# Order of the small fp32 and fp32r matrix products in a hybrid attention block: outputs grouped by type, transposes taken in pairs

## The chip, the cores and the metric

The kernel runs on one core of one Trainium2 chip. The metric is the device time of one execution in microseconds (us); less is better. The time of the kernel before is the median of three runs. One further execution was taken with the hardware profiler; times "in the trace" count from the start of its span.

Engines are named as the profile does: PE is TensorE's matrix products and PEld its weight loads, DVE is VectorE, ACT ScalarE, POOL GpSimd, SP SyncE, which issues most DMA transfers.

## What is computed

One decoder layer on 272 tokens (16 meta tokens and 256 inputs) of width 2048, in fp32: a normalised input goes through one wide projection; two token mixers work side by side; their outputs are gated, summed and projected; then comes an MLP. The change touches the two mixers only. Cut from the reference:

```python
def gated_linear_attention(q, k, v, g):          # 4 heads, key width 256, value width 512, chunks of 64
    b = jnp.cumsum(gc, axis=3)
    q_dec = qc * jnp.exp(b)
    k_inv = kc * jnp.exp(-b)
    k_end = kc * jnp.exp(b_last - b)
    a = jnp.where(causal, jnp.einsum('bhnck,bhnsk->bhncs', q_dec, k_inv), 0.0)
    o_intra = jnp.einsum('bhncs,bhnsv->bhncv', a, vc)
    ...
def forgetting_attention(q, k, v, f_logit, b_forget):   # 8 heads of width 128
    s = jnp.einsum('bhqd,bhkd->bhqk', qh, kh) * scale + c[q] - c[k]
    p = jax.nn.softmax(jnp.where(mask, s, MASK_VALUE), axis=-1)
    outs.append(jnp.einsum('bhqk,bhkd->bhqd', p, vh))
```

The kernel writes the first as a quadratic attention over all 256 queries with decays folded into keys and queries: a score matrix at0/at1/az times the values.

## The kernel before

**Precision.** Large products are made from split operands: a number is cut into a high part in the type fp32r (a copy on ScalarE) and the rest (a subtraction on VectorE), and three, or for some shapes two, fp32r products are added up in PSUM. Small products are made in plain fp32; each of these shows as two records in the trace (its weights in two halves). A transpose is a product with the identity and shows as one record.

**The stream.** TensorE works through 128-column blocks of the weights. For each, `next_weights` loads two halves (SP), copies the high part `whi` (ScalarE, L120) and subtracts to get `wlo` (VectorE, L121); there are five buffers of halves. `gemm_all` (L148, L150, L152) makes 48 products of 272 columns for all tokens into a PSUM tile `psa`; `gemm2` (L143, L144) makes 16 pairs of 512 and 256 columns into `ps`. Both draw on a pool of three PSUM banks (`pg`); small products draw on one of five (`px`).

**The order.** Work between the large products is registered with `later(n, fn)`: `fn` is written into the program after the n-th following large product (`issued()` counts). From this program a scheduling pass makes the order of each engine's instructions, and an instruction may be placed earlier or later than it was written; the order is fixed when the kernel is built, and each engine takes its instructions in that order.

**A head of the linear attention** (`gla_head`) uses, in order: two key blocks, two query blocks (for head 0 the first key block and the queries come from the start-up stage), four value blocks, and for heads 1 to 3 four gate blocks. Its small work:

- `keys` (L519, L521) reads the key block's PSUM tile and writes the scaled keys `kx` and `kz`; L534, L538 and L540 scale queries and keys further (`qx`, `kx`).
- `scores` (L557, ten fp32 products into `pa`), registered with `later(3)` ahead of the value blocks.
- each value block i is read from PSUM into `vT` (L598, VectorE; the tag `vT` has two buffers, so the third block's write waits until the first block's transposes have read theirs), and `turn(i)` (L586, L587; for the last block also L590) transposes it into the PSUM tiles p0 and p1.
- `outputs` (L612, and L201 to L203 by way of `three`, L620), `sums` and `scale`.

`decays(hd)` (L415 to L446), one for each head, makes the factors `eb_all` and `en_all` that the keys and queries are multiplied with, by a long row of ScalarE and VectorE operations; head 0's runs while head 0's value blocks are on TensorE.

**A head of the softmax attention** (`fox_head`) uses a key, a query and a value block. `turn_v` (L769, L770) transposes the values, `turn_p` (L779 to L781) the probabilities, `out_v` (L201 to L203, L788) multiplies them.

Of the kernel before, what the change touches and what calls it, by code (L numbers as in the profile page):

```python
# [16 lines left out]
P = 128  # L17
# [3 lines left out]
NT = 256  # L21
# [44 lines left out]
def trunk(ctx: ExitStack, tc: tile.TileContext, hT, w_small, w_all, consts, w_alpha2, out):  # L66
    nc = tc.nc
    serial = [0]

    def nm(s):  # L70
        serial[0] += 1
        return f"{s}_{serial[0]}"
# [7 lines left out]
    px = ctx.enter_context(tc.tile_pool(name="px", bufs=5, space=PSUM))  # L80
# [3 lines left out]
    def bank(pool, s):  # L84
        return pool.tile([P, 512], F32, tag="bank", name=nm(s))
# [4 lines left out]
    def later(n, fn):  # L90
        waiting.append([n, fn])
# [33 lines left out]
    def next_weights(keep_hi=None):  # L125
        c = chunk[0]
        chunk[0] += 1
        parts = []
        for i in range(2):
            hi, lo, step = weight_half(c, i, None if keep_hi is None else keep_hi[:, HK * i : HK * (i + 1), :])  # L130
            step(0, HK)
            parts.append((hi, lo))
        return lambda k: (parts[k // HK][0][:, k % HK, :], parts[k // HK][1][:, k % HK, :])
# [29 lines left out]
    def gemm_all(w):  # L163

        ps = bank(pg, "psa")
        for k in range(KT):
            hi, lo = w(k)
            mac3(ps, hi, lo, k, k == 0, k == KT - 1)
        join(ps)
        issued()  # L170
        return ps
# [15 lines left out]
    def split_to(dst_hi, dst_lo, src):  # L187
        nc.scalar.copy(dst_hi, src)
        nc.vector.tensor_tensor(dst_lo, src, dst_hi.bitcast(F32), op=ALU.subtract)

    def split(pool, tag, src, bufs=None):

        kw = {} if bufs is None else {"bufs": bufs}
        hi = pool.tile(list(src.shape), F32R, tag=tag + "h", name=nm(tag + "h"), **kw)
        lo = pool.tile(list(src.shape), F32R, tag=tag + "l", name=nm(tag + "l"), **kw)
        split_to(hi, lo, src)
        return hi, lo

    def three(out, lhs, rhs, first, last):

        nc.tensor.matmul(out, lhs[0], rhs[0], start=first, stop=False)  # L201
        nc.tensor.matmul(out, lhs[0], rhs[1], start=False, stop=False)
        nc.tensor.matmul(out, lhs[1], rhs[0], start=False, stop=last)  # L203
# [279 lines left out]
    def padded(pool, name, cols, dtype=F32):  # L483
        t = pool.tile([P, cols], dtype, name=name)
        nc.gpsimd.memset(t if dtype == F32 else t.bitcast(F32), 0.0)
        return t

    Q1 = 2 * C - NM
    NB = NA - 4 * C
    at0 = padded(lin, "at0", NT)  # L490
    at1 = padded(lin, "at1", NT - Q1)
    vg = padded(lin, "vg", P)
    az = padded(lin, "az", 4 * NB)
    v0 = [lin.tile([P, GLA_DV], F32R, name=n) for n in ("v0h", "v0l")]
# [8 lines left out]
    def gla_head(hd, sg, ready=None):  # L503
# [74 lines left out]
        v1 = att.tile([P, GLA_DV], F32, tag="v1", name=nm("v1"))  # L578
# [3 lines left out]
        def turn(i, vT):  # L582
            if not pv:
                pv.extend(bank(px, s) for s in ("p0", "p1"))
            cols = slice(P * i, P * (i + 1))
            nc.tensor.transpose(pv[0][:, cols], vT[:, 0:P], ident)  # L586
            nc.tensor.transpose(pv[1][:, cols], vT[:, P : 2 * P], ident)  # L587
            if i == 3:
                p2 = bank(px, "p2")[:, 0:P]
                nc.tensor.transpose(p2, vg, ident)  # L590
                split_to(*v0, pv[0])
                nc.scalar.copy(v1, pv[1])
                nc.scalar.copy(vz, p2)

        for i in range(4):
            ps = gemm_all(next_weights())
            vT = tmp.tile([P, NA], F32, tag="vT", name=nm("vT"))
            nc.vector.tensor_tensor(vT, ps[:, 0:NA], rb, op=ALU.mult)  # L598
            nc.gpsimd.tensor_copy(vg[:, NB * i : NB * (i + 1)], vT[:, 4 * C :])
            later(1, lambda i=i, vT=vT: turn(i, vT))  # L600


        oT = att.tile([P, 4, NT], F32, tag="oT", name=nm("oT"))
# [4 lines left out]
        def outputs():  # L608
            a0 = split(att, "a0", at0)
            cz = so[:, 3, 0 : 4 * NB]  # L610
            pz = bank(px, "po")[:, 0 : 4 * NB]
            nc.tensor.matmul(pz, vz, az, start=True, stop=True)  # L612
            nc.scalar.copy(cz, pz)
            for i in range(2):
                po = bank(px, "po")
                for j in range(2):
                    v = slice(P * (2 * i + j), P * (2 * i + j + 1))
                    o = po[:, NT * j : NT * (j + 1)]
                    three(o, [e[:, v] for e in v0], a0, True, False)
                    nc.tensor.matmul(o[:, Q1:], v1[:, v], at1, start=False, stop=True)  # L620
                pj = po.rearrange("p (j t) -> p j t", t=NT)
                zj = pj[:, :, NT - NB :]
                nc.vector.tensor_tensor(zj, zj, cz.rearrange("p (j t) -> p j t", t=NB)[:, 2 * i : 2 * i + 2, :],
                                        op=ALU.add)
                nc.scalar.copy(oT[:, 2 * i : 2 * i + 2, :], pj)
                nc.scalar.activation(so[:, 2 * i : 2 * i + 2, :], pj, AF.Square)
            nc.gpsimd.tensor_tensor(so[:, 0:2, :], so[:, 0:2, :], so[:, 2:4, :], op=ALU.add)
            nc.gpsimd.tensor_tensor(so[:, 0, :], so[:, 0, :], so[:, 1, :], op=ALU.add)
# [4 lines left out]
        def scale():  # L633
            for i in range(4):
# [4 lines left out]
                split_to(og_tile()[:, j, 0, :], og_tile()[:, j, 1, :], oT[:, i, :])  # L639

        later(2, outputs)
        later(3, sums)
        if sg is None:
# [36 lines left out]
    for hd in range(GLA_H):  # L680
        later(1 + 3 * hd, lambda hd=hd: with_table(decays, hd))
    later(3 * GLA_H - 1, lambda: with_table(forget))
    gla_head(0, sg0, (qd0, first_ps[NF - 1]))
    for hd in range(1, GLA_H):
        gla_head(hd, None)
# [27 lines left out]
    def fox_head(hd):  # L713
# [38 lines left out]
        vT = tmp.tile([P, NA], F32, tag="vT", name=nm("vT"))  # L752
# [56 lines left out]
                      for o in range(2))  # L809
            split_to(hi, lo, og4)  # L810

        later(1, turn_v)
        later(2, turn_p)
        later(3, out_v)
        if four == 3:
# [2 lines left out]
    for hd in range(FOX_H):  # L818
        fox_head(hd)
# [97 lines left out]
    for n in range(NL):  # L917
        j, ps = KT - NL + n, bank(pg if n < 3 else px, "ps")
# [149 lines left out]
```

## Time and profile before

| | |
|---|---|
| median of three runs | 1538.71 us (1538.29 to 1539.51) |
| the profiled execution | 1538.62 us |
| its span, first to last instruction | 1536.8 us |
| granted TensorE clock, mean | 0.999 |
| instructions of the four compute engines and weight loads | 25427 |
| first output product (L612) of heads 0 and 3 of the linear attention | 95.0 and 292.4 us into the span |
| first score product (L736) of the softmax heads, last product of their last correction (L805) | 326.8 and 479.1 us |

The page of the profile gives busy time by engine, the chain of work that ended last, and the costliest groups. A matmul's record is longer than the time for which it holds TensorE: it includes the way through the array, and the next one starts before it ends. So costs of small products are read from the distance between starts, and the record's length only where two records are drawn together ("x2").

The stretch that the change touches ends at about 479 us. In it TensorE is busy nearly throughout; the gaps between large products hold the small ones: the outputs of head 3 run from 292.44 to 294.97 us, the transposes of one value block hold a gap of a few tenths of a microsecond.

### The profile page before, as it was taken

The page shows a single profiled execution, that of the slowest core. Times are in us where ns is not written, and L with a number is a line of the kernel's source. Part 1 is how long each engine was busy: PE and PEld are TensorE (multiplying, and loading weights), DVE is VectorE, ACT ScalarE, POOL GpSimd, SP SyncE. Part 2 cuts the span into 40 slices and gives each one's busy share as a digit, 9 for nine tenths or more (in the row PEclk, how much of TensorE's full clock was granted, in tenths as well). Part 3 has the DMA queues.
Part 4 walks back from the last instruction along what each step waited for, and adds up shares of the span by engine and source line. Part 5 has one row for each costly group of instructions (what it writes and reads, how often), then busy time and mean ns, then how long its engine had stood idle before and what let it go on. Part 6 is the DMA issues. An engine that isn't in the chain of part 4 may idle for free.

```text
span 1536.8 us, 25427 instructions
## 1 busy us (share of the span) xinstructions
PE 1525.6 (99%) x9812; PEld 1402.4 (91%) x9812; DVE 1059.5 (69%) x1659; ACT 789.6 (51%) x1271; POOL 127.6 (8%) x213
## 2 busy tenths in 40 slices
PE   9999999999999999999999999999999999999997
PEld 8999999999999999999999899999999999999997
DVE  7898858586666656556777876567765776667765
ACT  6766444555545444444655554445444454444563
POOL 6012000011100000000011000000000000000022
PEclk9999999999999999999999999999999999999999
DMA  9455545465555655666565556666565666656652
GB/s 325 165 165 165 182 161 188 157 210 173 167 166 182 201 195 199 197 198 200 182 212 195 193 195 201 195 200 196 194 202 196 201 196 197 199 195 201 192 192 101
DMA packets 86602, 293.09 MB, mean 191 GB/s; under 512 B 9112, under 2 KB 16800, under 8 KB 86352
## 3 DMA queue, kind: packets, MB, share of 16 engines
q1 hardware_dynamic: 85872, 289.62, 57.6%
q8 instruction: 77, 1.26, 0.3%
q0 software_dynamic: 176, 1.12, 0.2%
q10 hardware_dynamic: 432, 0.72, 0.1%
q14 instruction: 45, 0.37, 0.1%
HBM read 289.32 MB, written 2.11 MB: 190 GB/s over the span
## 4 chain that ended last, share of the span: by engine, by line
PE 97%; DVE 1%; ACT 1%; issue 0%; POOL 0%; DMA 0%; POOLq 0%; ACTq 0%; DVEq 0%
PE ps L143 51%; PE ps L144 26%; PE psa L152 5%; PE psa L148 5%; PE psa L150 4%; PE ps L359 1%; PE ps L361 1%; PE ps L937 1%; PE pa L557 1%; PE ps L921 0%; DVE wlo L121 0%; ACT whi L120 0%; PE po L620 0%; DMA h<-hT_dram 0%; POOL o L985 0%
## 5 line engine op out<-in xcount | busy, mean ns | idle before, releaser
L121 DVE TENSOR_TENSOR wlo<-raw,whi 128x1024 fp32r<-128x1024 f32 x522 | 640.3, 1227 | 400.0 <-ACT whi L120 390.8
L120 ACT CAST whi<-raw 128x1024 fp32r<-128x1024 f32 x522 | 546.9, 1048 | 604.7 <-PE ps L143 534.0
L143 PE MATMUL ps<-x,whi 128*128 128x512 f32 x1952 | 656.4, 382 | 0.8 <-DVE x L874 0.8
L144 PE MATMUL ps<-x,wlo 128*128 128x256 f32 x1952 | 535.3, 274 | 0.0
L143 PEld LDWEIGHTS ps<-x,whi 128*128 128x128 f32 x1952 | 366.4, 188 | 64.2 <-DVE x L874 1.1
L144 PEld LDWEIGHTS ps<-x,wlo 128*128 128x128 f32 x1952 | 366.4, 188 | 0.1
L143 PE MATMUL ps<-a,whi 128*128 128x512 f32 x960 | 320.0, 380 | 0.0
L144 PE MATMUL ps<-a,wlo 128*128 128x256 f32 x960 | 262.4, 274 | 0.0
L143 PEld LDWEIGHTS ps<-a,whi 128*128 128x128 f32 x960 | 179.9, 188 | 30.8
L148 PE MATMUL psa<-x,whi 128*128 128x272 f32 x640 | 182.5, 286 | 0.0
L152 PE MATMUL psa<-x,whi 128*128 128x272 f32 x640 | 180.8, 283 | 0.0
L144 PEld LDWEIGHTS ps<-a,wlo 128*128 128x128 f32 x960 | 180.2, 188 | 0.3
L150 PE MATMUL psa<-x,wlo 128*128 128x272 f32 x624 | 176.3, 283 | 0.0
L148 PEld LDWEIGHTS psa<-x,whi 128*128 128x128 f32 x640 | 120.0, 187 | 0.3
L152 PEld LDWEIGHTS psa<-x,whi 128*128 128x128 f32 x640 | 120.0, 187 | 0.0
L150 PEld LDWEIGHTS psa<-x,wlo 128*128 128x128 f32 x624 | 117.2, 188 | 0.0
L862 POOL TENSOR_TENSOR acc<-acc,hsq 128x256 f32<-128x256 f32 x26 | 28.4, 1092 | 736.4 <-ACT hsq L861 736.4
L143 PE MATMUL ps<-og,whi 128*128 128x512 f32 x256 | 85.8, 380 | 0.0
L143 PE MATMUL ps<-y,whi 128*128 128x512 f32 x256 | 85.3, 380 | 0.0
L144 PE MATMUL ps<-og,wlo 128*128 128x256 f32 x256 | 70.2, 274 | 0.0
L144 PE MATMUL ps<-y,wlo 128*128 128x256 f32 x256 | 70.0, 274 | 0.0
L184 DVE TENSOR_TENSOR evt<-ps,evb 128x256 f32<-128x256 f32 x158 | 65.9, 417 | 0.5 <-ACT evb L181 0.5
(297 smaller groups left out, 1420.9 us busy)
## 6 DMA issues: line engine op xcount, KB each, us to landing
raw<-w_all_dram SPq DMA_DIRECT2D x537, 512.0 KB, 4.3
raw<-w_all_dram SPq DMA_DIRECT2D x8, 384.0 KB, 6.7
h<-hT_dram SPq DMA_DIRECT2D x8, 275.0 KB, 6.8
negc<-fdram POOLq DMA_DIRECT2D x1, 1088.0 KB, 7.9
out_dram<-o SPq DMA_DIRECT2D x2, 512.0 KB, 2.6
raw<-w_all_dram SPq DMA_DIRECT2D x2, 256.0 KB, 3.7
room<-w_small_dram SPq DMA_DIRECT2D x1, 320.0 KB, 7.9
out_dram<-o ACTq DMA_DIRECT2D x1, 320.0 KB, 3.0
```

The costliest lines, as they stand in the source:

```text
L120: nc.scalar.copy(hi[:, k, :], r)
L121: nc.vector.tensor_tensor(lo[:, k, :], r, hi[:, k, :].bitcast(F32), op=ALU.subtract)
L143: nc.tensor.matmul(steps(ps), hi, steps(row(x)), start=first, stop=False)
L144: nc.tensor.matmul(steps(ps[:, 0:NT]), lo, steps(x[:, 0, :]), start=False, stop=last)
L148: nc.tensor.matmul(steps(ps[:, X_LO]), hi, steps(x_lo[:, k]), start=first, stop=False, skip_group_check=True)
L150: nc.tensor.matmul(steps(ps[:, 0:NA]), lo, steps(x_hi[:, k]), start=False, stop=last and hi is None, skip_group_check=True)
L152: nc.tensor.matmul(steps(ps[:, 0:NA]), hi, steps(x_hi[:, k]), start=False, stop=last, skip_group_check=True)
L184: nc.vector.tensor_tensor(t, ps[:, 0:NT], b, op=ALU.add)
L359: nc.tensor.matmul(steps(ps), hi, steps(row(x[:, k])), start=st, stop=False)
L361: nc.tensor.matmul(steps(ps[:, 0:NT]), lo, steps(x[:, k, 0]), start=False, stop=sp)
L557: nc.tensor.matmul(dst, k[:, a], q[:, a, :], start=(a == 0), stop=(a == 1))
L862: nc.gpsimd.tensor_tensor(acc, acc, sq, op=ALU.add)
```

## The change

Three edits, with no change to what is computed:

1. The transposes of value blocks 0 and 2 wait for one more large product, so that blocks 0 and 1, and blocks 2 and 3, are transposed in the same gap.
2. `outputs` makes all twelve fp32r products of a head first, into two PSUM tiles (`pos`), then the fp32 product `pz` and then the four fp32 products with `at1`. Only the first product into a tile's bank carries the start flag. Before, each of the four output quarters had three fp32r products followed by its fp32 product, and `pz` came first.
3. `turn_v` of the softmax heads waits for one more large product and so comes into the gap of `turn_p`.

```diff
-            later(1, lambda i=i, vT=vT: turn(i, vT))
+            later(2 - i % 2, lambda i=i, vT=vT: turn(i, vT))
...
             a0 = split(att, "a0", at0)
             cz = so[:, 3, 0 : 4 * NB]
+            pos = [bank(px, "po") for _ in range(2)]
+            parts = [(slice(P * n, P * (n + 1)), pos[n // 2][:, NT * (n % 2) : NT * (n % 2 + 1)], n % 2) for n in range(4)]
+            for v, o, j in parts:
+                for n, (e, b) in enumerate(((v0[0], a0[0]), (v0[0], a0[1]), (v0[1], a0[0]))):
+                    nc.tensor.matmul(o, e[:, v], b, start=(j == 0 and n == 0), stop=False, skip_group_check=True)
             pz = bank(px, "po")[:, 0 : 4 * NB]
             nc.tensor.matmul(pz, vz, az, start=True, stop=True)
             nc.scalar.copy(cz, pz)
-            for i in range(2):
-                po = bank(px, "po")
-                for j in range(2):
-                    v = slice(P * (2 * i + j), P * (2 * i + j + 1))
-                    o = po[:, NT * j : NT * (j + 1)]
-                    three(o, [e[:, v] for e in v0], a0, True, False)
-                    nc.tensor.matmul(o[:, Q1:], v1[:, v], at1, start=False, stop=True)
+            for v, o, j in parts:
+                nc.tensor.matmul(o[:, Q1:], v1[:, v], at1, start=False, stop=True, skip_group_check=True)
+            for i, po in enumerate(pos):
                 pj = po.rearrange("p (j t) -> p j t", t=NT)
...
-        later(1, turn_v)
+        later(2, turn_v)
         later(2, turn_p)
```

The scheduling pass makes new orders from this. Three places follow. Names carry their buffer's number; lines behind the output products are one higher in the changed kernel.

TensorE in head 0, before, at the end of the fourth value block (`psa_136_1036`). `psa_150_1110` is the first key block of head 1:

```order
L152 MATMUL psa_136_1036<-x_81,whi_134_1031 128x4x17x4
L586 MATMUL p0_112_902<-cons_82,vT_129_1021 128x128
L587 MATMUL p1_113_903<-cons_82,vT_129_1021 128x128
L148 MATMUL psa_150_1110<-x_81,whi_145_1099 128x4x17x4
L150 MATMUL psa_150_1110<-x_81,wlo_146_1100 128x4x17x4
```

Thirty products into that key block later, still before, the scores stand:

```order
L152 MATMUL psa_150_1110<-x_81,whi_148_1105 128x4x17x4
L557 MATMUL pa_128_1001<-qx_79_663,kx_77_661 64x48
L148 MATMUL psa_150_1110<-x_81,whi_148_1105 128x4x17x4
L150 MATMUL psa_150_1110<-x_81,wlo_149_1106 128x4x17x4
L557 MATMUL pa_128_1001<-qx_79_663,kx_77_661 64x48
L557 MATMUL pa_128_1001<-qx_79_663,kx_77_661 64x64 x2
```

The same place now; in brackets the engine whose semaphore the instruction waits for. `vT_103_835` and `vT_112_902` are value blocks 0 and 1, `psa_150_1108` is the key block of head 1:

```order
L152 MATMUL psa_136_1036<-x_81,whi_134_1031 128x4x17x4
L557 MATMUL pa_126_997<-qx_79_663,kx_77_661 64x48 [waits DVE_49]
L586 MATMUL p0_127_1015<-cons_82,vT_103_835 128x128 [waits DMAHW1_49]
L587 MATMUL p1_128_1016<-cons_82,vT_103_835 128x128
L586 MATMUL p0_127_1015<-cons_82,vT_112_902 128x128
L587 MATMUL p1_128_1016<-cons_82,vT_112_902 128x128
L557 MATMUL pa_126_997<-qx_79_663,kx_77_661 64x48 [waits DVE_49]
L557 MATMUL pa_126_997<-qx_79_663,kx_77_661 64x64 x2
L557 MATMUL pa_126_997<-qx_79_663,kz_78_662 64x16 [waits Pool_49]
L557 MATMUL pa_126_997<-qx_79_663,kz_78_662 64x16 [waits DVE_49]
L148 MATMUL psa_150_1108<-x_81,whi_145_1097 128x4x17x4 [waits Activation_49]
```

The first score product has moved from inside the key block to directly behind the fourth value block, ahead of the transposes of the first two value blocks; the key block's 48 products all come behind the ten small score products.

VectorE in head 0, before, in the queue ahead of the `kx` that these scores read (`half_92_745`, `room_83`, `ends_538` belong to `decays`, `vT_129_1021` is value block 2):

```order
L440 TENSOR_TENSOR room_83<-room_83,half_92_745 128x2x256
L598 TENSOR_TENSOR vT_129_1021<-psa_121_921,rb_534 128x272
L436 TENSOR_TENSOR ends_538<-ends_538 128x2
L121 TENSOR_TENSOR wlo_155_1174<-raw_153_1172,whi_154_1173 128x1024
L424 TENSOR_SCALAR room_83<-pz_123_973,cons_82 128x272
```

and now:

```order
L440 TENSOR_TENSOR room_83<-room_83,half_92_745 128x2x256
L436 TENSOR_TENSOR ends_538<-ends_538 128x2
L121 TENSOR_TENSOR wlo_155_1174<-raw_153_1172,whi_154_1173 128x1024
L424 TENSOR_SCALAR room_83<-pz_121_969,cons_82 128x272
L424 TENSOR_SCALAR room_83<-pz_122_970,cons_82 128x272
```

The read of value block 2 has left this place; it now stands behind both L519 and L540, and waits for TensorE. The other operations up to `kx` are the same, with one weight split and one small addition (L176) in another place among them.

TensorE at the outputs of head 1, before (`po_1885` here is the tile of `pz`):

```order
L612 MATMUL po_1885<-az,vz_1443 128x64
L201 MATMUL po_1888<-a0h_1881,v0h 128x256
L202 MATMUL po_1888<-a0l_1882,v0h 128x256
L201 MATMUL po_1900<-a0h_1881,v0h 128x256
L203 MATMUL po_1888<-a0h_1881,v0l 128x256
L620 MATMUL po_1888<-at_545,v_193_1442 128x144
L201 MATMUL po_1888<-a0h_1881,v0h 128x256
L202 MATMUL po_1888<-a0l_1882,v0h 128x256
L203 MATMUL po_1888<-a0h_1881,v0l 128x256
L620 MATMUL po_1888<-at_545,v_193_1442 128x144
```

and now, the end of the same row:

```order
L615 MATMUL po_1886<-a0h_1881,v0h 128x256
L615 MATMUL po_1886<-a0l_1882,v0h 128x256
L615 MATMUL po_1886<-a0h_1881,v0l 128x256
L617 MATMUL po_1899<-az,vz_1443 128x64
L620 MATMUL po_1885<-at_545,v_193_1442 128x144 x2
L620 MATMUL po_1886<-at_545,v_193_1442 128x144 x2
L143 MATMUL ps_1933<-x,whi_1922 128x4x32x4
```

The five fp32 products of the head (L617, four times L620) stand together behind the twelve fp32r ones.

## The prediction

> **What bounds the kernel now.** I read the page first: busy times, then the chain of work that ended last.
>
> ```profile
> PE 1525.6 (99%) x9812; PEld 1402.4 (91%) x9812; DVE 1059.5 (69%) x1659; ACT 789.6 (51%) x1271; POOL 127.6 (8%) x213
> PE 97%; DVE 1%; ACT 1%; issue 0%; POOL 0%; DMA 0%; POOLq 0%; ACTq 0%; DVEq 0%
> ```
>
> TensorE is the bound: whatever is added to its row, work or idle time, is added to the span, and nothing later can take it back. So the next view is the one of waits, for TensorE alone.
>
> ```profile
> PE warm L323 <- DVE ones L208: 1.3, 1, 1.3
> PE ps L143 <- DVE x L874: 0.8, 1, 0.8
> PE pn L961 <- ACT sq L942: 0.7, 1, 0.7
> PE ps L359 <- ACT whi L292: 0.4, 1, 0.4
> PE pa L557 <- DVE kx L519: 0.3, 1, 0.3
> ```
>
> Of these five waits one lies where the change works: the first score product of head 0 (L557) waits for VectorE's scaled keys kx (L519). The window view of the stretch ahead of it shows why (the columns are length, then busy time of TensorE, weight load, VectorE, ScalarE, GpSimd, then granted clock):
>
> ```profile
> 67.60:83.80 16.20, 15.86 (x128) 15.42 (x127) 15.92 (x33) 12.24 (x23) 3.66 (x4) 1.00 0.50 164
> ```
>
> VectorE is busy 15.92 of 16.20 us. It is an average of 69% over the kernel, but here it has a queue with no room, and what stands in that queue ahead of kx sets when kx exists. TensorE is full as well only because the order gives it other products until then.
>
> **The change at that place.** TensorE now, in order of time (timeline):
>
> ```profile
> 73.29 0.33 PE L586 MATMUL p<-cons,vT 128*128 128x128 f32 x1
> ...
> 79.33 0.29 PE L152 MATMUL psa<-x,whi 128*128 128x272 f32 x1
> 79.45 0.27 PE L586 MATMUL p<-cons,vT 128*128 128x128 f32 x1
> 79.56 0.27 PE L587 MATMUL p<-cons,vT 128*128 128x128 f32 x1
> 79.59 0.37 PE L148 MATMUL psa<-x,whi 128*128 128x272 f32 x1
> 79.80 0.29 PE L150 MATMUL psa<-x,wlo 128*128 128x272 f32 x1
> ...
> 83.23 0.29 PE L152 MATMUL psa<-x,whi 128*128 128x272 f32 x1
> 83.82 0.31 PE L557 MATMUL pa<-qx,kx 128*64 128x48 f32 x2 [0.30 <-DVE kx L519]
> 84.06 0.39 PE L148 MATMUL psa<-x,whi 128*128 128x272 f32 x1
> 84.29 0.28 PE L150 MATMUL psa<-x,wlo 128*128 128x272 f32 x1
> 84.50 0.56 PE L557 MATMUL pa<-qx,kx 128*64 128x48 f32 x6
> ```
>
> The fourth value block of head 0 ends at 79.45. Then come two transposes and 30 products of the next head's first key block, 79.59 to 83.35, and only then the scores. In the changed order (shown above) the first score product stands directly behind the fourth value block, ahead of all 48 products of that key block. TensorE takes its matmuls in order, so those products can no longer cover the time until kx. VectorE:
>
> ```profile
> 72.80 0.43 DVE L598 TENSOR_TENSOR vT<-psa,rb 128x272 f32<-128x272 f32 x1
> ...
> 77.22 0.43 DVE L598 TENSOR_TENSOR vT<-psa,rb 128x272 f32<-128x272 f32 x1
> 77.57 0.15 DVE L436 TENSOR_TENSOR ends<-ends 128x2 f32<-128x2 f32 x1
> ...
> 83.35 0.42 DVE L519 TENSOR_TENSOR kx<-ps,en_all 128x256 f32<-128x256 f32 x1
> ```
>
> *When TensorE gets there.* A pair of transposes with its change of type costs 79.80 − 79.45 − 0.12 (the L148's own, from 79.33 to 79.45 for the same shape) = 0.23 us. Three pairs stood ahead of 79.45, the third just behind it; the first, at the end of the second block, goes, but its 0.23 turns into waiting: the fourth block's first product needs the buffer that the L598 of 72.80 + 0.43 = 73.23 empties, the same event for which the L586 of 73.29 waits now. The second pair's 0.23 is gained. So the fourth block ends at 79.45 − 0.23 = 79.22.
>
> *When kx is there.* The same queue stands ahead of kx, less the L598 of 77.22, which now waits for transposes: 77.57 − 77.22 = 0.35 us. kx is written by 83.35 + 0.42 − 0.35 = 83.42, and L557 starts 0.05 later, as now (83.77, 83.82): 83.47.
>
> *The stall* is 83.47 − 79.22 = 4.25 us. Now it is 83.82 − (83.23 + 0.12) = 0.47. With the first pair's 0.23 turned into waiting: 4.25 − 0.47 + 0.23 = **+4.0 us**. Behind it TensorE has its usual work. ScalarE and VectorE come out further ahead of it, which helps nothing. If VectorE's reordered small operations cost or save 0.1, so does the stall; from 3.8 to 4.2.
>
> **What it saves.** Scores: two records alone now take 84.29 − 0.12 − 83.82 = 0.35; the ten that follow take 85.41 − 0.12 − 84.50 = 0.79, 0.08 each:
>
> ```profile
> 85.19 0.39 PE L152 MATMUL psa<-x,whi 128*128 128x272 f32 x1
> 85.41 0.28 PE L148 MATMUL psa<-x,whi 128*128 128x272 f32 x1
> ```
>
> In the new order they follow each other among other fp32 products: 0.35 − 0.16, **−0.2** (0 to −0.3).
>
> Outputs, four heads:
>
> ```profile
> 292.44 0.33 PE L612 MATMUL po<-az,vz 128*128 128x64 f32 x2
> ...
> 292.77 0.29 PE L202 MATMUL po<-a0l,v0h 128*128 128x256 f32 x1
> 292.89 0.28 PE L201 MATMUL po<-a0h,v0h 128*128 128x256 f32 x1
> ...
> 293.73 0.41 PE L620 MATMUL po<-at,v 128*128 128x144 f32 x2
> ...
> 294.10 0.28 PE L203 MATMUL po<-a0h,v0l 128*128 128x256 f32 x1
> ```
> ```profile
> L620 PE MATMUL po<-at,v 128*128 128x144 f32 x32 | 6.5, 286 | 0.0
> ```
>
> An fp32 product with the fp32r one behind it takes 294.10 − 293.73 = 0.37; less the fp32r product's 0.12 (292.77 to 292.89) that is 0.25. Its two records of 286 ns lie 0.41 − 0.29 = 0.12 apart, so without a change of type it would take 0.24 to 0.25. A change of type there costs 0.00 to 0.015 us: the thing that the edit removes is nearly free. L612 is dearer: 292.77 − 292.44 − 0.12 = 0.21 for 64 columns, which by L620's 0.25 for 144 are worth 0.11. Its 0.10 over is weight load that so short a product doesn't hide; between fp32r and fp32 it keeps none to all of it, and I take 0.04 off. Per head four changes of 0.0125 and 0.04: 0.09, times four **−0.36** (−0.1 to −0.6).
>
> Transposes: a pair's 0.23 less two transposes at 79.56 − 79.45 = 0.11 leaves 0.015 for a gap. By the order eight gaps fewer in the linear attention (three of head 0, where the pairs go behind the scores, one of head 1, two each of heads 2 and 3) and seven in the softmax attention (the first head keeps two): 15 × 0.015 = **−0.22** (0 to −0.4).
>
> The copies and splits that move on other engines (ScalarE's vah, vb and at copies; VectorE's v0l, a0l, og) I cost at nothing. The window view of head 1 shows the cover: TensorE is busy 44.00 of 44.00 us although VectorE is busy for 42.41, because the weights are split ahead of their use.
>
> ```profile
> 96.00:140.00 44.00, 44.00 (x332) 42.24 (x332) 42.41 (x91) 25.65 (x50) 11.18 (x12) 1.00 0.50 163
> ```
>
> If that cover failed, each late copy or split (the L598 above took 0.43) would show in full.
>
> Sum: 4.0 − 0.2 − 0.36 − 0.22 = **+3.2 us**. The profiled execution took 1538.62 (span 1536.8), 0.09 under the median of 1538.71: 1541.8 for it, 1541.9 beside the median. With all bounds at their ends +2.5 to +4.1: 1541.2 to 1542.8.
>
> **Rivals.** *The clock falls in the stall.* The window view of the end of the kernel:
>
> ```profile
> 1526.20:1529.60 3.40, 2.28 (x18) 1.90 (x17) 1.47 (x6) 1.80 (x6) 1.79 (x2) 1.00 0.60 243
> 1529.60:1533.00 3.40, 0.00 (x0) 0.00 (x0) 3.02 (x8) 0.30 (x1) 1.59 (x2) 1.00 0.34 126
> 1533.00:1536.80 3.80, 0.00 (x0) 0.00 (x0) 0.00 (x0) 0.00 (x0) 0.00 (x0) 0.50 0.59 222
> ```
> ```profile
> 1528.66 0.49 PE L961 MATMUL pn<-sq,ones 128*128 128x128 f32 x2 [0.67 <-ACT sq L942]
> ```
>
> After the last product's end (1529.15) the clock stood at 1.00 for 3.85 us and then at 0.50. The new gap, from the last product's end at about 79.1 + 0.3 to 83.47, is 4.1 us, a little longer. At half clock the products of a stretch cost their time again. How long the clock stays low is bounded by the start of the program, where the eight 256-column records of L323 lie some 0.45 us apart, double the 0.22 of two 128-column transposes:
>
> ```profile
> 1.28 3.78 PE L323 MATMUL warm<-ones 128*128 128x256 f32 x8 [1.28 <-DVE ones L208]
> 6.95 1.22 PE L359 MATMUL ps<-x,whi 128*128 128x512 f32 x4
> ```
>
> Between 2.6 us (a window of 3.4 partly spent waiting) and 5.7 (1.28 to 6.95) of low clock cost half: 1.3 to 2.9, about 2.2, so **1544.1**. Against it: two thirds of a window busy (2.28 of 3.40) kept the clock, and the gap is at the edge. The Trainium skill, "TensorE: Matmul & The Clock Gate", section "What's actually happening", says that TensorE's clock goes to half after one idle window of about 3.4 us, and that the windows run freely; the trace agrees, half came 3.85 us after the last product. By that page a gap of 4.1 us holds a whole window in about one phase of five, an estimate from its figure.
>
> *No stall (the other side).* If kx were ready by 79.2, the 0.47 would go and the savings stay: 1538.71 − 0.47 − 0.2 − 0.36 − 0.22 = **1537.5**, no measurable change. It decides where VectorE reaches L519 4.2 us sooner; for it speaks that one operation leaves its queue, against it that this is 0.35 us and that the queue has no idle time to give up.
>
> *A second wait.* The third block's L598 now waits until the first block's transposes have read their buffer. Behind it in VectorE's queue stand two scans, the fourth block's L598 and the last part of the queries, for which the wide scores wait; in the later heads the transposes come after scores of 2.1 us.
>
> ```profile
> 126.58 2.11 PE pa L557 x20
> ```
>
> In head 0 VectorE reaches that L598 at about 86.5, long after the transposes. In heads 1 to 3 it would wait some 2 us; if weight splits behind it came late, 1 us a head: **1545**. TensorE's gap-free 44 us above, with VectorE as full, speak against it.
>
> **How the numbers follow.** Forecast 0.50, clock 0.28, no stall 0.15, second wait 0.07. Time: 1541.9; its own range 1541.2 to 1542.8. The range of 8 in 10 goes from 1540.0 (part of the stall covered) to 1545.0. About 0.2%, 3.1 us, is what a measurement of this kernel can tell from no change, and the forecast of +3.2 lies on that line, so its half is split: 0.27 slower, 0.23 same. Slower: 0.27 + 0.28 + 0.07 = 0.62. Same: 0.23 and most of the no-stall case, 0.35. Faster: 0.03.
>
> **What would show it.** In the changed profile the list of TensorE's waits has one new large row, L557 on DVE kx, about 4 us, near 79; VectorE's L519 near 83.0; no gap at the output products or the transposes; and granted clock 1.00 behind the stall (0.50 for some us would be the rival). The forecast is wrong if L557's wait is under 3 us, if the softmax heads' joint transposes show waits, or if the outputs save more than 0.2 us a head.

## The result and the profile after

The changed kernel took 1545.41 us in the median of six runs (1543.87 to 1545.85); the kernel before, six runs as well, 1538.80 (1538.24 to 1539.60). The ratio is 1.004, with a 95% interval of 1.0029 to 1.005: slower, by 6.6 us in the medians, where +3.2 was forecast. The profiled execution took 1545.51 with a span of 1543.7 us.

The page's busy times and the list of TensorE's waits (us in total, times, the longest), changed kernel:

```profile
PE 1528.3 (99%) x9812; PEld 1404.5 (91%) x9812; DVE 1060.1 (69%) x1659; ACT 790.6 (51%) x1271; POOL 128.3 (8%) x213
```
```profile
PE pa L557 <- DVE kx L519: 4.1, 1, 4.1
...
PE psa L148 <- DVE vT L598: 0.3, 1, 0.3
```

The row of 4.1 is new, and so is the small one below it: the fourth value block's first product now waits for the buffer for which a transpose waited before. TensorE's timeline there (start, length, engine and line, operation, and in brackets the idle time and who ended it):

```profile
78.53 0.28 PE L152 MATMUL psa<-x,whi 128*128 128x272 f32 x1
82.90 0.45 PE L557 MATMUL pa<-qx,kx 128*64 128x48 f32 x2 [4.09 <-DVE kx L519]
...
86.36 0.43 PE L148 MATMUL psa<-x,whi 128*128 128x272 f32 x1
86.59 0.43 PE L150 MATMUL psa<-x,wlo 128*128 128x272 f32 x1
...
90.05 0.28 PE L148 MATMUL psa<-x,whi 128*128 128x272 f32 x1
90.17 0.28 PE L150 MATMUL psa<-x,wlo 128*128 128x272 f32 x1
```

and VectorE's:

```profile
82.43 0.42 DVE L519 TENSOR_TENSOR kx<-ps,en_all 128x256 f32<-128x256 f32 x1
...
85.85 0.43 DVE L598 TENSOR_TENSOR vT<-psa,rb 128x272 f32<-128x272 f32 x1
```

The stall is 82.90 − (78.53 + 0.12) = 4.25 us. Behind it the large products do not run as usual: at 86.4 one starts 0.23 after another, at 90 it is 0.12. The windows of that stretch say why (length, busy times of TensorE, weight load, VectorE, ScalarE, GpSimd, then the granted clock); they are laid out in steps of 3.41 us, at whose ends this trace's clock changes:

```profile
75.93:79.34 3.41, 2.88 (x25) 2.67 (x23) 3.35 (x9) 2.51 (x5) 0.00 (x0) 1.00 0.46 161
79.34:82.75 3.41, 0.00 (x0) 0.00 (x0) 3.41 (x8) 1.81 (x4) 1.14 (x1) 1.00 0.43 135
82.75:86.17 3.42, 3.27 (x19) 2.81 (x20) 3.42 (x11) 0.00 (x0) 0.00 (x0) 0.50 0.44 153
86.17:89.58 3.41, 3.41 (x17) 3.41 (x17) 2.95 (x10) 0.00 (x0) 0.82 (x2) 0.50 0.50 154
89.58:92.99 3.41, 3.41 (x30) 3.41 (x30) 1.29 (x2) 2.23 (x4) 0.00 (x0) 1.00 0.01 2
```

A granted clock of 0.50 for 6.83 us, just behind the stall, which the busy share hides: TensorE counts as busy while it runs at half speed.

**Where the 6.9 us of span lie.** Both kernels make the same 9440 large products, so the traces can be laid side by side product by product. Product 300 starts at 52.53 us before and 51.96 after, product 1000 (in head 2's first key block, behind all small work of heads 0 and 1 that the change moves) at 160.35 and 166.57, product 9200 (late in the MLP) at 1496.70 and 1503.17; the spans end at 1536.84 and 1543.72. So −0.57 had come about by product 300, ahead of everything that the change moves (in the other traces this difference is about −0.6 to +0.4), **+6.79** comes between 300 and 1000, +0.25 between 1000 and 9200, and +0.41 at the end.

The last stretch is no measure of a kernel: in the executions below it is longer than in the trace of before by 0.01 to 2.43 us, with no pattern (late weights and an activation among the last products of the MLP). It and the start-up may well be most of the scatter of some 2 us between runs of one kernel; runs without a trace cannot show it. The two middle stretches repeat within about 0.1 us where kernels share the edits that act there (e9 and e10: +4.05 and +4.06; after product 1000 the eight kernels with all the later edits: +0.20 to +0.26), and the experiments are read from them:

| | product 300 to 1000 | 1000 to 9200 | median, and that of before beside it | ratio (95%) |
|---|---|---|---|---|
| the change | +6.79 | +0.25 | 1545.41, 1538.80 | 1.0040 (1.0029 to 1.0050) |
| e1 value blocks' transposes alone | +6.62 | −0.36 | 1545.30, 1539.11 | 1.0038 (1.0025 to 1.0050) |
| e2 outputs alone | −0.04 | 0.00 | 1539.20, 1539.11 | 0.9999 (0.9990 to 1.0008) |
| e3 softmax heads' transposes alone | −0.03 | +0.45 | 1539.35, 1539.11 | 1.0002 (0.9993 to 1.0011) |
| e4 wait filled | +4.69 | +0.20 | 1543.97, 1539.11 | 1.0034 (1.0021 to 1.0046) |
| e5 scores one gap later | −0.10 | +0.26 | 1538.92, 1538.49 | 1.0001 (0.9992 to 1.0009) |
| e6 a quarter filled | +7.01 | +0.25 | 1544.79, 1538.49 | 1.0041 (1.0029 to 1.0054) |
| e7 half filled | +5.47 | +0.26 | 1543.79, 1538.49 | 1.0033 (1.0021 to 1.0046) |
| e8 head 0 as before | −0.10 | +0.20 | 1538.58, 1538.49 | 1.0000 (0.9991 to 1.0008) |
| e9 25 products | +4.05 | +0.21 | 1543.32, 1538.52 | 1.0031 (1.0019 to 1.0043) |
| e10 30 products | +4.06 | +0.26 | 1543.54, 1538.52 | 1.0032 (1.0020 to 1.0044) |
| e11 pairs in heads 1 to 3 alone | −0.21 | −0.35 | 1538.39, 1538.52 | 0.9997 (0.9989 to 1.0006) |

### The profile page after: what moved, and what is told of

It is laid out like the page before. It is cut to its first block, busy times and chain, and to the rows that moved or that the text cites. A ratio compares the mean times of both kernels' runs of the same rounds, so it can differ in the third digit from the quotient of the medians.

```text
span 1543.7 us, 25426 instructions
## 1 busy us (share of the span) xinstructions
PE 1528.3 (99%) x9812; PEld 1404.5 (91%) x9812; DVE 1060.1 (69%) x1659; ACT 790.6 (51%) x1271; POOL 128.3 (8%) x213
## 4 chain that ended last, share of the span: by engine, by line
PE 97%; DVE 1%; ACT 1%; issue 0%; DMA 0%; POOL 0%; SPq 0%; POOLq 0%; DVEq 0%; ACTq 0%
PE ps L143 50%; PE ps L144 26%; PE psa L148 5%; PE psa L152 5%; PE psa L150 4%; PE ps L359 1%; PE ps L938 1%; PE ps L361 1%; PE pa L557 1%; PE ps L922 1%; DMA raw<-w_all_dram 0%; PE po L615 0%; DVE wlo L121 0%; ACT whi L120 0%; PE po L620 0%
```

## The experiments

### Which of the three edits it is: e1, e2, e3

Each has one edit of the change and nothing else: e1 `later(2 - i % 2, ...)` for `turn`, e2 the new `outputs`, e3 `later(2, turn_v)`.

> Only the transposes of a gated head's value blocks two to a gap; outputs and value transposes of the other heads as before. Theory A (the pairing alone holds head 0's scores up, and the clock falls in the wait): L557 waits for DVE kx about 4.1 us near 79, the clock record shows 0.50 for one or two stretches of 3.4 us behind it, time 1545 (1543.5 to 1546). Rival B (a part of the loss comes with the joined outputs or the joined value transposes): the same wait, but 1 us or more under the changed kernel, 1544 or less at two stretches of half clock. Rival C (the loss is elsewhere): no wait near 79, about 1538.5.

> Only the gated heads' outputs, first all fp32r and then all fp32. Theory A: no wait at L557, clock 1.00, and 4 x 0.03 to 0.09 us less: 1538.4 to 1538.8, not told from before. Rival B: over 1539.5, with a gap of some tenths of a us before L615 or L617 in each of the four heads.

> Only the value transposes of the other twelve heads joined two to a gap. Theory A: 12 gaps fewer at about 0.01 us each, so 1538.6 (1538.2 to 1539.2), clock 1.00, no wait over 1 us that before does not have. Rival B: 0.5 us or more above before, as the changed kernel loses 0.5 us over these heads in its one profiled execution.

e1 has nearly the whole loss, 6.62 of 6.79 us in the first stretch. Its list of TensorE's waits, and its windows:

```profile
PE pa L557 <- DVE kx L519: 4.0, 1, 4.0
```
```profile
79.05:82.46 3.41, 0.30 (x3) 0.10 (x1) 3.35 (x9) 2.54 (x5) 0.58 (x1) 1.00 0.49 154
82.46:85.87 3.41, 2.53 (x16) 2.11 (x16) 3.41 (x10) 0.00 (x0) 0.56 (x1) 0.50 0.45 137
85.87:89.29 3.42, 3.42 (x17) 3.38 (x16) 3.39 (x11) 0.00 (x0) 0.82 (x2) 0.50 0.50 170
```

The wait and the two stretches of half clock are there as in the changed kernel; from product 1000 on it gains 0.36.

e2 gains nothing in either stretch. Its order of the outputs is not the change's, though: in e2 the short product (L617, before L612) still stands among fp32r products, as the scheduling pass did not put it where it is written, while in the change it stands behind all twelve in every head. Head 3's outputs in e2, then in the change:

```profile
292.56 0.33 PE L617 MATMUL po<-az,vz 128*128 128x64 f32 x2
...
292.91 0.28 PE L615 MATMUL po<-a0h,v0h 128*128 128x256 f32 x1
...
293.74 1.14 PE L620 MATMUL po<-at,v 128*128 128x144 f32 x8
294.63 0.48 PE L143 MATMUL ps<-x,whi 128*128 128x512 f32 x1
```
```profile
298.37 0.28 PE L615 MATMUL po<-a0h,v0h 128*128 128x256 f32 x1
...
299.81 0.33 PE L617 MATMUL po<-az,vz 128*128 128x64 f32 x2
299.98 1.20 PE L620 MATMUL po<-at,v 128*128 128x144 f32 x8
300.92 0.48 PE L143 MATMUL ps<-x,whi 128*128 128x512 f32 x1
```

In e2 the short product has not lost its price: with the one fp32r product between the two starts taken off, 292.91 − 292.56 − 0.12 = 0.23, where it was 0.21. From the first output product to the next large one the head takes 294.63 − 292.08 = 2.55 us in e2 (292.08 is the first L615), and 300.92 − 298.37 = 2.55 in the change, where the types are grouped as planned; before it was 294.97 − 292.44 = 2.53. So neither order gains.

e3 costs 0.45 us by the trace, which its eleven runs cannot tell from nothing. A softmax head's transposes in the trace of before, where two gaps hold them:

```profile
367.15 0.29 PE L152 MATMUL psa<-x,whi 128*128 128x272 f32 x1
...
367.41 0.48 PE L143 MATMUL ps<-x,whi 128*128 128x512 f32 x1
367.73 0.28 PE L144 MATMUL ps<-x,wlo 128*128 128x256 f32 x1
...
372.76 0.27 PE L144 MATMUL ps<-x,wlo 128*128 128x256 f32 x1
...
373.11 0.37 PE L148 MATMUL psa<-x,whi 128*128 128x272 f32 x1
373.32 0.28 PE L150 MATMUL psa<-x,wlo 128*128 128x272 f32 x1
```

and in e3's trace, where one does:

```profile
372.99 0.28 PE L144 MATMUL ps<-x,wlo 128*128 128x256 f32 x1
...
373.57 0.37 PE L148 MATMUL psa<-x,whi 128*128 128x272 f32 x1
373.77 0.28 PE L150 MATMUL psa<-x,wlo 128*128 128x272 f32 x1
```

Start to start, less what the two large products take undisturbed: before (367.73 − 367.15 − 0.12 − 0.22) + (373.32 − 372.76 − 0.11 − 0.12) = 0.24 + 0.33; joined 373.77 − 372.99 − 0.11 − 0.12 = 0.55. A gap fewer saves 0.02, as forecast (0.015). The loss is not in the gaps: the 272-column products between them start 0.0004 us further apart on the mean, 0.36 us for the 866 of them between products 1700 and 3100. After product 1000 each trace with this edit loses (+0.20 to +0.45), and e1, e2 and e11, without it, do not. Why stays open.

### Is it the order? e5, e8

e5 leaves the pairs and lets head 0's scores wait one large product longer; e8 leaves head 0 as it was before and keeps the rest of the change.

```diff
-        later(3, scores)
+        later(4 if ready else 3, scores)
```
```diff
-            later(2 - i % 2, lambda i=i, vT=vT: turn(i, vT))
+            later(1 if ready else 2 - i % 2, lambda i=i, vT=vT: turn(i, vT))
```

> The changed kernel, but head 0's scores are due one gap later than they were, so that 32 products of head 1's first key block stand between the last value block and L557. Theory A (the loss is the order, TensorE set to wait for kx with nothing else ahead): L557 comes at about 83.1, the wait is 0 to 0.5 us, clock 1.00, time 1538.0 (1537.5 to 1538.8). Rival (the paired transposes come late for the buffers vT and pv, whatever stands before L557): the key block's products themselves wait 1 us or more for a bank or for DVE, time 1539.5 or more.

> The changed kernel, but the gated head that stands first transposes its value blocks one to a gap, as before. Theory A: no wait at L557, clock 1.00, and the savings that are left: 1538.3 (1537.8 to 1538.9). Rival B (joined outputs or value transposes cost): 1539.3 or more.

Both end the loss. In e5 the pairs of blocks 0 and 1 stand behind the third block, 32 products of the next key block are back ahead of L557, and the wait is 0.26 us:

```profile
83.58 0.32 PE L557 MATMUL pa<-qx,kx 128*64 128x48 f32 x2 [0.26 <-DVE kx L519]
```

So transposing in pairs costs nothing that these times show by itself; it cost because the order that came of it left TensorE nothing to do until kx. e8's time is before's within its interval.

### Is it the wait or the clock? e4, e6, e7, e9, e10

These keep the changed kernel's order and give TensorE work to do in its wait: products of ones with ones into columns of the value block's bank that nobody reads, 40, 10, 20, 25 and 30 of them. kx comes no sooner, so the stall costs what it cost, but TensorE stands idle for less of it. Line numbers are two higher in these kernels (L559 is L557); L170 is the filling.

```diff
+        for _ in range(fill):
+            nc.tensor.matmul(ps[:, 300:508], ones_r[:, 0:P], ones_r[:, 0:208], start=False, stop=False, skip_group_check=True)
...
-            ps = gemm_all(next_weights())
+            ps = gemm_all(next_weights(), 40 if ready and i == 3 else 0)
```

> The changed kernel with 40 fp32r products of 208 columns behind head 0's last value block, into columns of its bank that nobody reads, about 3.7 us of work that fills the 4.1 us in which TensorE waited. They take no work away: kx comes when it came. Theory A (the clock falls since TensorE stands idle): the wait at L557 shrinks to under 0.6 us, the clock record stays at 1.00 and the time is the changed kernel's less the half clock, 1542.0 (1541.6 to 1542.5). Rival (the clock falls for another reason there, or what follows is late for its data): the time stays at 1545, with 0.50 in the clock record or new waits behind L557.

> The changed kernel with 10 fp32r products of 208 columns behind the last value block: about 0.9 us of work, so that TensorE stands idle for about 3.1 us in place of 4.1. If the clock falls only where a whole stretch of 3.41 us is idle: 1.00 in every run, 1542.0. If part of a stretch is enough: 0.50 in some or all runs, 1543.7 to 1545.5.

> The changed kernel with 20 such products: about 1.8 us of work, idle for about 2.2 us. If only a whole idle stretch of 3.41 us lowers the clock, 1.00 in every run and 1542.0; if half a stretch is enough, mean clock 0.996 to 0.998 and 1543.7 to 1545.5 in some runs.

> The changed kernel with 25 products of 208 columns behind the last value block, none behind the scores: 2.7 us of work, a wait of about 1.3 us left. The traces so far fit a clock that is set anew every 3.41 us, to half where TensorE was busy for 0.48 of the 3.41 us before or less, and kept where it was 0.57 or more. A wait of 1.3 us leaves 0.6 busy at worst: no 0.50 behind the wait in any run, and 1538.8 + 4.1 - 0.0 = 1542.9 (1542.4 to 1543.5). Rival (any wait over 1 us lowers the clock in some runs, or the rest of the loss is not the clock): runs at 1544.3 and more beside the others.

> The same with 30 products: a wait of about 0.8 us left and no product behind the scores (e4 had six there, 0.7 us). Clock 1.00 behind the wait in every run, 1542.9 (1542.4 to 1543.5): TensorE's wait alone, by which the half clock is worth 1545.4 - 1542.9 = 2.5 us. Rival (the wait itself costs less and something behind it more): a time at or under 1542, or over 1544.

The timeline of e10:

```profile
79.41 0.28 PE L152 MATMUL psa<-x,whi 128*128 128x272 f32 x1
79.53 3.50 PE L170 MATMUL psa<-ones 128*128 128x208 f32 x30
83.79 0.32 PE L559 MATMUL pa<-qx,kx 128*64 128x48 f32 x2 [0.76 <-DVE kx L521]
```

The first score product comes 83.79 − 79.53 = 4.26 us after the value block, as without the filling, and the clock stays at 1.00 there. (It is at 1.00 in the profiled execution; in all twelve runs of e9 and e10 the mean granted clock is 0.998 or 0.999, as in before, against 0.996 or 0.997 in every run of e1 and e6.) From product 300 to 1000 the loss is 4.06, in e9 4.05. That is the price of the stall alone; the half clock is the rest, 6.79 − 4.06 = **2.73 us**. By the medians it is 6.61 less 4.80 (e9) or 5.02 (e10), 1.6 to 1.8, inside the scatter: the end of the span was 0.9 us long in the profiled e9 and e10 and 0.41 in the change. The traces decide here; the times alone would not have (the ratios' intervals overlap). e9's median lies in its range; e10's lies 0.04 above its own, and four of the twelve runs (1544.32 in e9, 1544.06 to 1544.45 in e10) lie past the lines that the rivals drew. Their clock of 0.998 and the long end of the profiled ones speak against a second loss, but only the profiled ones have a trace.

e4 missed its expectation of 1542.0. Its clock stayed at 1.00 and its wait shrank to 0.3, but the scheduling pass put six of the 40 products behind the scores:

```profile
79.05 3.94 PE L170 MATMUL psa<-ones 128*128 128x208 f32 x34
...
84.83 0.90 PE L170 MATMUL psa<-ones 128*128 128x208 f32 x6
85.56 0.30 PE L148 MATMUL psa<-x,whi 128*128 128x272 f32 x1
```

They take 85.56 − 84.83 = 0.73 us that the others do not have; of this 4.69 − 4.06 = 0.63 shows in its stretch. The expectation had also put the half clock at 3.4, half of the low stretch, which is too much: from L557 to the next large product the change takes 85.51 − 82.90 = 2.61 us at half clock and e10 85.31 − 83.79 = 1.52 at full: the small products take 1.7 times as long, not twice.

e6 and e7 show how little idle time is enough. Their windows, in steps of 3.41 us from where the clock was set, e6 first, then e7:

```profile
80.26:83.67 3.41, 0.53 (x6) 0.30 (x4) 3.41 (x10) 1.40 (x3) 1.14 (x1) 1.00 0.31 97
83.67:87.08 3.41, 3.41 (x20) 3.04 (x20) 3.41 (x10) 0.00 (x0) 0.24 (x1) 0.50 0.50 160
87.08:90.50 3.42, 3.42 (x17) 3.42 (x16) 2.50 (x9) 0.00 (x0) 0.52 (x2) 0.50 0.45 150
```
```profile
81.69:85.10 3.41, 1.64 (x18) 1.23 (x17) 3.41 (x11) 0.42 (x2) 1.14 (x1) 1.00 0.22 67
85.10:88.52 3.42, 3.42 (x19) 3.38 (x18) 3.42 (x10) 0.00 (x0) 0.56 (x1) 0.50 0.61 194
88.52:91.93 3.41, 3.41 (x30) 3.41 (x30) 2.21 (x8) 1.89 (x3) 0.20 (x1) 1.00 0.20 74
```

and e9, with a wait of 1.3:

```profile
81.15:84.56 3.41, 2.08 (x20) 1.68 (x20) 3.41 (x11) 0.56 (x2) 1.14 (x1) 1.00 0.16 54
84.56:87.98 3.42, 3.42 (x32) 3.39 (x31) 3.42 (x9) 0.00 (x0) 0.00 (x0) 1.00 0.60 201
```

With 0.53 or 1.64 of 3.41 us busy the clock is 0.50 next; with 2.08 it stays. The rival that only a wholly idle stretch lowers it falls with e6, and with e7 for a wait of 1.8 us. In e7 the profiled execution, with one low stretch, took 1545.84; four of its six runs took 1543.1 to 1544.0, as if the wait had there been cut in two by a stretch's end. Those four have a mean clock of 0.998, the two at 1545.5 and more 0.997. They have no trace, so this is inferred. In the same way two of the change's six runs (1543.87 and 1544.10) have 0.998 where the other four have 0.996 or 0.997; they may have had one low stretch in place of two, which no trace shows.

### What is left to win: e11

> The kernel before with the transposes of value blocks two to a gap in the gated heads 1 to 3 alone, outputs and the other heads as before: what is left of the change when head 0's order, the joined outputs (measured at no gain) and the joined value transposes of the other heads (measured at +0.3 to 0.5 us) are taken out. Theory: no wait at L557, clock 1.00, 0.3 us under before in the trace from product to product; the time 1538.2 to 1538.8 against 1538.5 to 1539.1 for before, too little for five runs to tell. Rival (even these pairs cost): 0.2 us or more over before in the trace.

The one part with a gain in the trace, −0.56 us from product 300 to 9200. Its time cannot be told from before's (0.9997, 0.9989 to 1.0006). No kernel here is shown to beat the one before.

## Why the prediction was right, and where it was not

**The stall: right.** Forecast 4.25 us, measured 4.25; that the hundredth agrees is luck, as the forecast left itself 0.2 either way and e1, with the same wait, has 83.34 − (79.08 + 0.12) = 4.14. L519 at 83.0, measured 82.43 in an execution that was 0.57 ahead by product 300. One pair of transposes turned into a wait of 0.3 for `vT`, as worked out (it was the pair that stood at 73.29, behind the third block; the one at the end of the second block was gained; two pairs, not three, stood ahead of 79.45; the sum is the same). The third block's L598 now comes at 85.85 (86.5 was given), and TensorE did not wait for it. The stall's net price with what is saved up to product 1000 is 4.06 (e10), where the terms gave 4.0 − 0.2 for the scores − 0.18 for the outputs of two heads − 0.06 for four gaps, 3.56. Of the 0.5 between them, 0.15 is the scores and 0.14 the outputs (below); the rest was not split further.

**The clock: the step that failed.** The 1545.41 lies 0.41 above the upper end of the range of 8 in 10, though none of the three signs of being wrong came. The forecast held the clock at 1.00 and gave its fall 0.28, because a gap of 4.1 us was "at the edge": two thirds of a window busy had kept the clock, a wholly idle one had lowered it, and what lies between was read as if only an idle window counted. The trace of before had no case between 0 and 2.28 of 3.40 us. In the profiled execution of the change one step was wholly idle, so that trace alone would fit the forecast's reading; e1 (0.30 busy), e6 and e7 decide. e7 is the nearest: 1.64 busy was too little. With that bound a gap of 4.1 us cannot be placed on the steps so as to spare the clock: of two neighbouring steps that share it, one has at least 2.05 us of it and so at most 1.36 busy. By that bound the fall was certain, and the case that was called a rival was the likeliest one. Its price was put at 2.2 us (1.3 to 2.9) and measured 2.73: the low clock lasted two stretches, not one and a part. With 2.73 in the sum the forecast would have been 1544.6; the 0.8 that is left is about the size of all the savings (0.78) that were forecast.

The Trainium skill, "TensorE: Matmul & The Clock Gate", section "What's actually happening", ties the fall to one idle window of about 3.4 us. The steps of 3.41 us agree with the traces; that the window must be idle does not: 0.48 of it busy (1.64 of 3.41) was not enough to keep the clock. The chance of one in five that was worked out from the page was wrong for this reason.

**The savings: mis-sized.** Scores, −0.2 forecast: the 0.35 and 0.79 of before hold what the product behind them starts late. Counted in the same way in e10, the first two records take 84.20 − 0.11 − 83.79 = 0.30 and the ten that follow 85.53 − 0.12 − 84.62 = 0.79, so about −0.05:

```profile
84.04 0.33 PE L588 MATMUL p<-cons,vT 128*128 128x128 f32 x1
84.20 0.27 PE L589 MATMUL p<-cons,vT 128*128 128x128 f32 x1
...
84.62 0.56 PE L559 MATMUL pa<-qx,kx 128*64 128x48 f32 x6
...
85.31 0.39 PE L148 MATMUL psa<-x,whi 128*128 128x272 f32 x1
85.53 0.29 PE L150 MATMUL psa<-x,wlo 128*128 128x272 f32 x1
```

Outputs: −0.36 forecast, −0.04 measured (e2), and 2.55 us for a head in the change's own order against 2.53. Nearly half of the forecast stood on the short product: in the change it moved behind the fp32r ones and brought nothing. Transposes of the value blocks in heads 2 and 3: −0.36 from product 1000 on (e1), where four gaps at 0.015 would be 0.06; −0.30 of it comes by product 1900, the rest at the start of the MLP, where e2 shows the same step; why it is so much stays open. Softmax heads: −0.1 forecast, +0.45 measured (e3), though each gap saved its 0.02. Alone these come to +0.09 after product 1000, together, in the change, to +0.25, where −0.34 had been forecast for this stretch.

**The other rivals.** No stall, and a second wait in heads 1 to 3, did not come: L557 has one large wait, and e1 gains in those heads. That the edits to the outputs cost or gain something was the rival in e1 to e3, and the traces exclude 0.2 us a head either way (2.55 and 2.55 against 2.53).

## What to carry to other kernels

Before small work is moved, ask which large products stand between it and the operand it waits for: here 30 products covered a queue on VectorE, and moving the transposes of two value blocks took them away. In this kernel, price an idle time of TensorE of about 2 us or more as the wait and then some 1.4 us of lost work for each stretch of 3.41 us at half clock behind it (2.73 for two). Where less than a microsecond is at stake and runs scatter by 2, lay two traces side by side product by product and leave out the start and the end.

## What the runs showed of the hardware

- TensorE's clock is set in steps of 3.41 us: in head 0 it was low for 3.41 us (e7) or for twice that (6.83, the change, e1 and e6). In the twelve traces of changed kernels and that of before, each step of which TensorE was busy for 0.48 or less was followed by 0.50 (0.00, 0.09, 0.16 and 0.48 in head 0; 0.00 to 0.48 at the end of the kernel), and each with 0.57 or more by 1.00, while the clock was at 1.00. The case of 0.57, at the end of the changed kernel:

```profile
1533.41:1536.82 3.41, 1.93 (x15) 1.55 (x14) 1.43 (x7) 2.10 (x6) 1.44 (x2) 1.00 0.70 285
1536.82:1540.24 3.42, 0.00 (x0) 0.00 (x0) 2.71 (x7) 0.00 (x0) 1.59 (x2) 1.00 0.35 125
```

- Once at 0.50, one step's work was not always enough to bring the clock back. The first low step of the change, e1 and e6, which holds the scores and four transposes, was followed by a second at 0.50 (busy 3.27, 2.53 and 3.41 of 3.41 by the records); that of e7, which holds the last few score products and otherwise large products, by 1.00. Whether some of the small instructions count for less was not tried.
- One low step cost 1.4 us (e7: 5.47 − 4.06) and two cost 2.73 (the change) or 2.95 (e6: 7.01 − 4.06): somewhat less than half of the 3.41 and 6.83 us that they last.
